# HGRN2 encoder layer on one core: x kept as rows until it is modulated, and the loads of the beginning in another order

## The chip, the cores and the metric

The kernel runs on 1 core of one Trainium2 chip. The metric is the time of one execution in microseconds on the device; lower is better. Times below are the median of three runs, and one execution was recorded by the hardware profiler.

## The reference

With DEPTH = 1 the trunk is one adaLN-modulated HGRN2 layer, then a final RMSNorm. It is applied to a prompt of 1024 rows and a sample of 256 rows (D = 1024, E = 2048, 16 heads).

```python
cs = jax.nn.silu(c)
shift, scale, gate = jnp.split(cs @ ada_w[0] + ada_b[0], 3, axis=-1)
h = _rms(x) * norm_g[0] * (1.0 + scale[:, None]) + shift[:, None]
q, f_fw, f_bw, i, z = jnp.split(h @ w_in, 5, axis=-1)
o = gated_chunkwise(q, ..., f_fw) + flip(gated_chunkwise(flip(q), ..., flip(f_bw)))
y = ((_rms(o) * norm_g_head) * jax.nn.silu(z)) @ w_out
x = x + gate[:, None] * y
return _rms(x) * final_g
```

## The kernel before, in words

The 1280 rows of x are ten row blocks of 128 (`xs[0]` to `xs[9]`), grouped in three segments `SEGS` of 512, 512 and 256 rows. The 1024 channels are eight blocks of 128; a channel pair r is blocks 2r and 2r+1. Everything later needs h with channels on the partitions, split into a high part `h_hi` and a low part `h_lo`, so that a product of fp32 accuracy is three fast ones: `hi*h_hi`, `hi*h_lo`, `lo*h_hi`. Weights are split in the same way by `split_w` (L113 to L119): ACT casts the high part, GpSimd subtracts for the low part. The high and low buffers are rings of three, the raw buffers a ring of two.

The program has three parts. The beginning (L229 to L327) makes h and, while h comes in, the products of the first two projections, q and ff of head 0. The main loop (L714 to L743) runs the other projections: the next one after the beginning is the value projection of heads 0 and 1 (`pv`, L444), ten tiles of 24 products. The tail is the output projection.

In the beginning, before the change, the order of all engines is the order of the code (`manual_schedule()`). A row block is loaded (`load_x`, ring of 4), normalised in place (`norm_x`: ACT square and root, DVE reciprocal and scaling), and transposed by TensorE into `xT` through PSUM (`transpose_x`; DVE copies one half, ACT the other). For a channel pair r, `mod_mm(r)` multiplies the conditioning by four pieces of `ada_w` (`aw`), `mod_tr(r)` transposes the result, and DVE finishes shift and scale (`mod`). `make_h(si, r)` then modulates `xT` in place, casts the high parts and subtracts the low ones. `first_project(r, accs)` adds a pair's products to the accumulators `p_acc[i, si]` (i = 0 for q, 1 for ff). Blocks 0 to 7 are transposed first, then come `mod_mm(0)` and the first products; the loop over r from 1 to 3 follows. Loads are issued by SP from the same code, so they stand between the blocks' work.

The eight PSUM banks have tags: `pj` (three), `tu` (two), `sc` (two) and `ob` (one). Before, the six accumulators take two `pj`, two `sc` and two `tu` banks, once the transposes are done.

```python
for r in range(1, 4):
    mod_mm(r)
    if r < 3:
        load_mod(r + 1)
    first_project(r - 1, ((0, 1),))
    mod_tr(r)
```

Of the kernel before, what the change touches and what calls it, by code (L numbers as in the profile page):

```python
# [45 lines left out]
def kernel(  # L46
# [99 lines left out]

    p0 = tc.alloc_tile_pool(name="p0", bufs=1)
    ada3 = ada_w[0].rearrange("(k p) n -> p k n", p=P)
    xT = [p0.tile([P, KT, sl], F32, name=f"xT{i}") for i, (_, sl) in enumerate(SEGS)]
    xts, p_acc, aws, raws, mrows = {}, {}, {}, {}, {}  # L150

    def load_x(j):
        xts[j] = p0.tile([P, D], F32, tag="xj", bufs=4, name=f"xj{j}")
        sp.dma_start(xts[j], xs[j])

    def load_mod(r, pieces=range(4)):

        for k0, i in [(0, 0), (0, 1), (4, 0), (4, 1)][pieces[0]:pieces[-1] + 1]:
            aws[r, k0, i] = p0.tile([P, 4, 256], F32, tag="aw", bufs=7, name=f"aw{r}_{k0}_{i}")
# [12 lines left out]

    def transpose_x(j):
        xj = xts[j]
        si = min(j // 4, 2)
        c = slice(j * P - SEGS[si][0], (j + 1) * P - SEGS[si][0])
        for h in range(2):
            xp = ps.tile([P, 512], F32, tag=("tu", "sc")[h], bufs=2, name=f"xp{j}_{h}")
            for i in range(4):
                k = 4 * h + i  # L180
                pe.transpose(xp[:, i * P:(i + 1) * P], xj[:, k * P:(k + 1) * P], ident)
            (act.copy if h else dve.tensor_copy)(
                xT[si][:, 4 * h:4 * h + 4, c], xp.rearrange("p (i c) -> p i c", i=4))
# [36 lines left out]
    def first_project(r, accs):  # L220

        for i, si in accs:
            hi, lo = ready[i]
# [4 lines left out]

    with tc.manual_schedule():  # L229
        crow = p0.tile([2 * KT, P], F32, name="crow")  # L230
        sp.dma_start(crow[:KT], c_prompt.rearrange("o (k p) -> (o k) p", p=P))
# [22 lines left out]
        def row(j):  # L254
            if j + 2 < 8:
                norm_x(j + 2)
            transpose_x(j)
            if j + 4 < NT:
                load_x(j + 4)

        norm_x(0)
        norm_x(1)
        for j in range(8):
            row(j)
            if j == 2:
                split(0, raws[0])
            if j == 3:
                load_mod(0)
                raws[1] = fetch_raw(1)
            if j == 5:  # L270
                load_mod(1, (0, 1, 2))
            if j == 6:
                split(1, raws[1])
        mod_mm(0)
        load_mod(1, (3,))
        mod_tr(0)
        make_h(0, 0)
        make_h(1, 0)
# [2 lines left out]
        norm_x(8)
        norm_x(9)
        first_project(0, ((0, 0), (1, 0)))
        row(8)
        row(9)
# [5 lines left out]
        for r in range(1, 4):
            mod_mm(r)
            if r < 3:
                load_mod(r + 1)
            first_project(r - 1, ((0, 1),))
            mod_tr(r)
            if r == 3:
                raws[2] = fetch_raw(2)
                wv = [split_w(*raws[2][0])]
            for si in range(3):  # L300
                make_h(si, r)
            first_project(r - 1, ((1, 1), (0, 2), (1, 2)))
            if r < 3:
                first_project(r, ((0, 0), (1, 0)))
        first_project(3, ((0, 0), (0, 1), (0, 2), (1, 0)))
# [540 lines left out]
```

## Time and profile before

| | us |
|---|---|
| median of three runs | 1708.84 |
| lowest, highest | 1707.33, 1713.25 |
| the profiled execution | 1708.66 |
| its span, first to last instruction | 1706.9 |
| TensorE busy | 1652.4 (97%) |
| DVE, ACT, GpSimd busy | 995.2, 803.0, 599.0 |
| mean granted TensorE clock | 0.993 |

The span is 1.8 us shorter than the execution's own time. A busy TensorE is not one at its peak: the granted clock tells which of its two levels it has, 1.2 GHz (0.50) or 2.4 GHz (1.00). In the rows, PE is TensorE, PEld its weight loads, POOL is GpSimd, and SP issues the loads.

### The profile page before, as it was taken

The page shows a single profiled execution, that of the slowest core. Times are in us where ns is not written, and L with a number is a line of the kernel's source. Part 1 is how long each engine was busy: PE and PEld are TensorE (multiplying, and loading weights), DVE is VectorE, ACT ScalarE, POOL GpSimd, SP SyncE. Part 2 cuts the span into 40 slices and gives each one's busy share as a digit, 9 for nine tenths or more (in the row PEclk, how much of TensorE's full clock was granted, in tenths as well). Part 3 has the DMA queues.
Part 4 walks back from the last instruction along what each step waited for, and adds up shares of the span by engine and source line. Part 5 has one row for each costly group of instructions (what it writes and reads, how often), then busy time and mean ns, then how long its engine had stood idle before and what let it go on. Part 6 is the DMA issues. An engine that isn't in the chain of part 4 may idle for free.

```text
span 1706.9 us, 28295 instructions
## 1 busy us (share of the span) xinstructions
PE 1652.4 (97%) x11511; PEld 1442.3 (84%) x11511; DVE 995.2 (58%) x2223; ACT 803.0 (47%) x1213; POOL 599.0 (35%) x547
## 2 busy tenths in 40 slices
PE   5999999999999999999999999999999999899998
PEld 4798789888988898889888998889888988788886
DVE  5647664757566745774576457644865476834322
ACT  6543634464545454544455445634563456542210
POOL 1533333343344333433344334433443334510000
PEclk8999999999999999999999999999999999999999
DMA  8312311011011011111111110111111100664310
GB/s 284 123 40 62 101 29 50 29 38 38 29 53 38 29 38 41 32 47 38 38 35 47 38 38 29 41 32 44 41 38 35 44 17 13 205 197 148 124 50 25
DMA packets 121268, 103.06 MB, mean 60 GB/s; under 512 B 3929, under 2 KB 108466, under 8 KB 121138
## 3 DMA queue, kind: packets, MB, share of 16 engines
q1 hardware_dynamic: 121138, 101.26, 18.9%
q8 instruction: 90, 1.47, 0.4%
q14 instruction: 40, 0.33, 0.1%
HBM read 85.50 MB, written 15.74 MB: 59 GB/s over the span
## 4 chain that ended last, share of the span: by engine, by line
PE 78%; DVE 9%; ACT 3%; POOL 3%; issue 2%; DMA 0%; DVEq 0%; POOLq 0%
PE pv L444 13%; PE y L690 13%; PE pff L422 13%; PE pfb L422 13%; PE pq L422 8%; PE pz L422 7%; PE ob L609 3%; DVE g L467 3%; PE up L532 3%; PE sc L553 2%; DVE kts L523 1%; PE kt L520 1%; DVE ku L474 1%; POOL wz_l L118 1%; PE sc L559 1%
## 5 line engine op out<-in xcount | busy, mean ns | idle before, releaser
L488 POOL TENSOR_TENSOR ku<-xx,dec 128x256 f32<-128x256 f32 (+1 forms) x96 | 82.0, 854 | 305.0 <-DVE dec L481 147.1
L444 PE MATMUL pv<-wv_h,h_hi 128*128 128x256 f32 x640 | 181.2, 283 | 0.0
L444 PE MATMUL pv<-wv_h,h_lo 128*128 128x256 f32 x640 | 181.1, 283 | 0.0
L444 PE MATMUL pv<-wv_l,h_hi 128*128 128x256 f32 x640 | 181.1, 283 | 0.0
L523 DVE COPY kts<-kt 128x512 f32<-128x512 f32 (+2 forms) x96 | 47.9, 499 | 198.0 <-PE kt L520 198.0
L422 PE MATMUL pz<-h_hi,wz_h 128*128 128x512 f32 (+1 forms) x384 | 144.4, 376 | 0.0
L422 PE MATMUL pq<-h_hi,wq_h 128*128 128x512 f32 (+1 forms) x360 | 139.1, 387 | 0.0
L422 PE MATMUL pff<-h_hi,wff_h 128*128 128x512 f32 (+1 forms) x360 | 138.5, 385 | 0.0
L422 PE MATMUL pfb<-h_hi,wfb_h 128*128 128x512 f32 (+1 forms) x384 | 136.3, 355 | 1.4 <-DVE q L406 1.4
L422 PE MATMUL pz<-h_hi,wz_l 128*128 128x512 f32 (+1 forms) x384 | 136.7, 356 | 0.0
L422 PE MATMUL pz<-h_lo,wz_h 128*128 128x512 f32 (+1 forms) x384 | 136.4, 355 | 0.0
L422 PE MATMUL pfb<-h_lo,wfb_h 128*128 128x512 f32 (+1 forms) x384 | 136.0, 354 | 0.0
L422 PE MATMUL pfb<-h_hi,wfb_l 128*128 128x512 f32 (+1 forms) x384 | 135.8, 354 | 0.0
L422 PE MATMUL pq<-h_hi,wq_l 128*128 128x512 f32 (+1 forms) x360 | 129.4, 359 | 0.0
L422 PE MATMUL pq<-h_lo,wq_h 128*128 128x512 f32 (+1 forms) x360 | 129.0, 358 | 0.0
L422 PE MATMUL pff<-h_hi,wff_l 128*128 128x512 f32 (+1 forms) x360 | 128.3, 356 | 0.0
L422 PE MATMUL pff<-h_lo,wff_h 128*128 128x512 f32 (+1 forms) x360 | 128.0, 356 | 0.0
L444 PEld LDWEIGHTS pv<-wv_l,h_hi 128*128 128x128 f32 x640 | 122.9, 192 | 0.0
L444 PEld LDWEIGHTS pv<-wv_h,h_lo 128*128 128x128 f32 x640 | 122.9, 192 | 0.0
L444 PEld LDWEIGHTS pv<-wv_h,h_hi 128*128 128x128 f32 x640 | 122.9, 192 | 0.0
L467 DVE TENSOR_TENSOR_SCAN g<-reset,g 128x512 f32<-128x512 uint8 (+1 forms) x96 | 101.8, 1073 | 24.6 <-ACT g L459 24.5
L397 POOL TENSOR_SCALAR k<-g,k_scale,k_bias 128x512 f32<-128x512 f32 (+1 forms) x96 | 75.0, 781 | 113.0 <-ACT g L395 104.3
(195 smaller groups left out, 4477.2 us busy)
## 6 DMA issues: line engine op xcount, KB each, us to landing
xj<-in_x_prompt_dram SPq DMA_DIRECT2D x16, 512.0 KB
wq_r<-in_hg_w_in_dram SPq DMA_DIRECT2D x16, 512.0 KB
aw<-in_ada_w_dram SPq DMA_DIRECT2D x16, 512.0 KB
wff_r<-in_hg_w_in_dram SPq DMA_DIRECT2D x16, 512.0 KB
wv_r<-in_hg_w_in_dram SPq DMA_DIRECT2D x16, 512.0 KB
wfb_r<-in_hg_w_in_dram SPq DMA_DIRECT2D x16, 512.0 KB
wz_r<-in_hg_w_in_dram SPq DMA_DIRECT2D x16, 512.0 KB
wo_r<-in_hg_w_out_dram SPq DMA_DIRECT2D x16, 512.0 KB
```

What stands on the lines that cost most here:

```text
L118: pool.tensor_tensor(lo, raw, hi.bitcast(F32), ALU.subtract)
L397: pool.tensor_scalar(k, g, k_scale[:, e:e + 1], k_bias[:, e:e + 1], ALU.mult, ALU.add)
L422: pe.matmul(acc[:, :sl], a[:, k, :], h[si][:, k, :], start=n == 0, stop=n == 3 * KT - 1)
L444: pe.matmul(acc[:, :2 * P], h[si][:, k, c], a[:, k % 4, :], start=n == 0, stop=n == 3 * KT - 1)
L467: dve.tensor_tensor_scan(gs, reset[:, :sl], gs, 0.0, ALU.mult, ALU.add)
L474: dve.tensor_tensor(chunks(ku), g3[:, :, last:last + 1].broadcast_to([P, nch, C]), g3, ALU.subtract)
L488: pool.tensor_tensor(u4[:, :, ca], x4[:, :, ca], dec[:, :, cb].broadcast_to([P, nb, C]), ALU.mult)
L523: dve.tensor_copy(kt[:, c], tp[:, c])
L532: pe.matmul(up[:, c], kt[:, c], v_t[e, b], start=True, stop=True)
L553: pe.matmul(sps[d][c * C:(c + 1) * C, i, c * C:(c + 1) * C], ke[:, o:o + C], qe[:, o:o + C], start=True, stop=True)
L609: pe.matmul(ob[:, c], l, r, start=n == 0, stop=n == len(ops) - 1)
L690: pe.matmul(y_bank(j, n), u[:, e % HALF, :], w[e][:, n * 512:(n + 1) * 512], start=first and e == 0, stop=last and e == NH - 1)
```

## The change

`xT`, `transpose_x` and the copies out of it are gone. A normalised row block stays as it is in its own buffer (ring of 10), and `make_h` now transposes what it needs, one channel block of one segment at a time, into a PSUM bank (`tu` for odd, `pj` for even channel blocks). ACT modulates from there straight into the high part, DVE modulates from there into a buffer `hv`, and the low part is `hv` less the high part, on GpSimd for even blocks and on DVE for odd ones. The accumulators of the sample segment share one bank `pf_2`, so one `tu` and one `pj` bank are left for the transposes. Only TensorE and SP keep the order of the code; a scheduler orders DVE, ACT and GpSimd by priority. The load list stands ahead of everything, with four pieces of modulation 1 ahead of row blocks 4 to 7, and the `aw` ring grows from 7 to 12. The lower-bound vector (`lbrow`) is loaded and transposed late. The second half of wv is split between the products instead of ahead of the last eighteen.

```diff
-        xts[j] = p0.tile([P, D], F32, tag="xj", bufs=4, name=f"xj{j}")
+        xts[j] = p0.tile([P, D], F32, tag="xj", bufs=10, name=f"xj{j}")
...
-        grp = 0 if SEGS[si][0] < TP else 1
-        hv = [xT[si][:, k, :] for k in (2 * r, 2 * r + 1)]
-        hi = [h_hi[si][:, k, :] for k in (2 * r, 2 * r + 1)]
-        lo = [h_lo[si][:, k, :] for k in (2 * r, 2 * r + 1)]
-        shift, scale = [[mod[:, s, k, grp:grp + 1] for k in (2 * r, 2 * r + 1)] for s in range(2)]
-        act.activation(hv[0], hv[0], AF.Identity, bias=shift[0], scale=scale[0])
-        dve.tensor_scalar(hv[1], hv[1], scale[1], shift[1], ALU.mult, ALU.add)
-        dve.tensor_copy(hi[0], hv[0])
-        act.copy(hi[1], hv[1])
-        pool.tensor_tensor(lo[0], hv[0], hi[0].bitcast(F32), ALU.subtract)
-        dve.tensor_tensor(lo[1], hv[1], hi[1].bitcast(F32), ALU.subtract)
+        s0, sl = SEGS[si]
+        grp = 0 if s0 < TP else 1
+        for k in (2 * r, 2 * r + 1):
+            xp = (tu_bank if k % 2 else pj_bank)(f"xp{si}_{k}")[:, :sl]
+            for i in range(sl // P):
+                pe.transpose(xp[:, i * P:(i + 1) * P], xts[s0 // P + i][:, k * P:(k + 1) * P], ident)
+            shift, scale = [mod[:, s, k, grp:grp + 1] for s in range(2)]
+            hi, lo = h_hi[si][:, k, :], h_lo[si][:, k, :]
+            hv = p0.tile([P, 512], F32, tag="hv", bufs=4, name=f"hv{si}_{k}")[:, :sl]
+            act.activation(hi, xp, AF.Identity, bias=shift, scale=scale)
+            dve.tensor_scalar(hv, xp, scale, shift, ALU.mult, ALU.add)
+            (dve if k % 2 else pool).tensor_tensor(lo, hv, hi.bitcast(F32), ALU.subtract)
...
-    with tc.manual_schedule():
+    with tc.manual_schedule(engines={PE, SP}):
...
         for j in range(4):
             load_x(j)
-        raws[0] = fetch_raw(0)
+        load_mod(0)
+        for i in range(2):
+            raws[i] = fetch_raw(i)
+        load_mod(1)
+        for j in range(4, 8):
+            load_x(j)
+        load_mod(2)
+        for j in range(8, NT):
+            load_x(j)
...
+        def products(r, si):
+            first_project(r, ((0, si), (1, si)))
+
+        for j in range(4):
+            norm_x(j)
+        mod_mm(0)
+        load_mod(3)
+        raws[2] = [fetch_raw(2)]
+        mod_tr(0)
+        split(0, raws[0])
+        split(1, raws[1])
+        make_h(0, 0)
+        products(0, 0)
+        mod_mm(1)
+        mod_tr(1)
+        for j in range(4, 8):
+            norm_x(j)
+        make_h(0, 1)
+        make_h(1, 0)
+        products(1, 0)
+        make_h(1, 1)
+        products(0, 1)
+        mod_mm(2)
+        products(1, 1)
+        mod_tr(2)
+        make_h(0, 2)
...
+        make_h(1, 2)
+        products(2, 0)
+        mod_mm(3)
+        make_h(2, 0)
+        products(2, 1)
+        mod_tr(3)
+        make_h(0, 3)
+        make_h(2, 1)
+        products(0, 2)
+        make_h(1, 3)
+        products(3, 0)
+        products(1, 2)
...
+        make_h(2, 2)
+        make_h(2, 3)
+        wv = [split_w(*raws[2][0][0])]
+        products(3, 1)
+        ready[2] = wv + [split_w(*raws[2][0][1])]
+        products(2, 2)
+        products(3, 2)
```

Three places show how the instructions moved. The first is ACT at the norms of row blocks 4 to 7 (`sq` is the square of a block, `rst` its root, `xp` a bank of transposes, `xT` the transposed x; the number behind a name is the block or segment). Before:

```order
L168 ACTIVATE sq4_188,ssum4_189<-xj4_165 128x1024
L169 ACTIVATE rst4_190<-ssum4_189,eps_t_71 128x1
L182 COPY xT0_98<-xp2_1_201 128x4x128
L117 CAST wq0_h_209<-wq0_r_120 128x1024
L168 ACTIVATE sq5_213,ssum5_214<-xj5_186 128x1024
L169 ACTIVATE rst5_215<-ssum5_214,eps_t_71 128x1
L182 COPY xT0_98<-xp3_1_226 128x4x128
L168 ACTIVATE sq6_244,ssum6_245<-xj6_207 128x1024
L169 ACTIVATE rst6_246<-ssum6_245,eps_t_71 128x1
L182 COPY xT1_99<-xp4_1_257 128x4x128
L168 ACTIVATE sq7_265,ssum7_266<-xj7_232 128x1024
L169 ACTIVATE rst7_267<-ssum7_266,eps_t_71 128x1
```

With the change:

```order
L168 ACTIVATE sq4_322,ssum4_323<-xj4_134 128x1024
L184 ACTIVATE h_hi0_89<-xp0_2_350,mod_81 128x512
L169 ACTIVATE rst4_324<-ssum4_323,eps_t_71 128x1
L168 ACTIVATE sq5_329,ssum5_330<-xj5_136 128x1024
L184 ACTIVATE h_hi0_89<-xp0_3_359,mod_81 128x512
L169 ACTIVATE rst5_331<-ssum5_330,eps_t_71 128x1
L168 ACTIVATE sq6_336,ssum6_337<-xj6_138 128x1024
L169 ACTIVATE rst6_338<-ssum6_337,eps_t_71 128x1
L168 ACTIVATE sq7_343,ssum7_344<-xj7_140 128x1024
L169 ACTIVATE rst7_345<-ssum7_344,eps_t_71 128x1
L184 ACTIVATE h_hi1_90<-xp1_0_368,mod_81 128x512
```

Between the norms stood copies of finished transposes; now there stand the modulating copies of channel blocks 2 and 3 of segment 0, which read `mod`, so the squares of blocks 5 to 7 come behind modulation 1.

The second is TensorE behind a modulation's small transpose (`pf0_0` is q's accumulator of segment 0). Before, at pair 0:

```order
L212 MATMUL mod_ps_130<-ident_66,mrow0_352 128x128
L226 MATMUL pf0_0_371<-h_hi0_89,wq0_h_209 128x512
L226 MATMUL pf0_0_371<-h_lo0_92,wq0_h_209 128x512
L226 MATMUL pf0_0_371<-h_hi0_89,wq0_l_210 128x512
L226 MATMUL pf0_0_371<-h_hi0_89,wq0_h_209 128x512
L226 MATMUL pf0_0_371<-h_lo0_92,wq0_h_209 128x512
```

With the change, behind the transposes for pair 1 of segment 0:

```order
L180 MATMUL xp0_3_359<-ident_66,xj3_112 128x128
L180 MATMUL xp1_0_368<-ident_66,xj4_134 128x128
L180 MATMUL xp1_0_368<-ident_66,xj5_136 128x128
L180 MATMUL xp1_0_368<-ident_66,xj6_138 128x128
L180 MATMUL xp1_0_368<-ident_66,xj7_140 128x128
L180 MATMUL xp1_1_377<-ident_66,xj4_134 128x128
L180 MATMUL xp1_1_377<-ident_66,xj5_136 128x128
L180 MATMUL xp1_1_377<-ident_66,xj6_138 128x128
L180 MATMUL xp1_1_377<-ident_66,xj7_140 128x128
L216 MATMUL pf0_0_165<-h_hi0_89,wq0_h_247 128x512
L216 MATMUL pf0_0_165<-h_lo0_92,wq0_h_247 128x512
L216 MATMUL pf0_0_165<-h_hi0_89,wq0_l_248 128x512
```

Products stood directly behind the modulation; now eight transposes of row blocks 4 to 7, for pair 0 of segment 1, stand ahead of pair 1's products of segment 0.

The third is ACT at the end of the beginning (`wv0_1` is the second half of wv, `q0` and `g0_0` the first results of q and ff). Before:

```order
L195 CAST h_hi1_90<-xT1_99 128x512
L192 ACTIVATE xT2_100<-xT2_100,mod_81 128x256
L195 CAST h_hi2_91<-xT2_100 128x256
L117 CAST wv0_1_h_742<-wv0_1_r_676 128x1024
L316 ACT_TABLE_LOAD
L316 ACTIVATE e0_758<-e0_758 128x16
L317 ACTIVATE e1_759<-e1_759 128x16
L117 CAST wfb0_h_891<-wfb0_r_889 128x1024
L405 ACTIVATE q0_0_792<-pf0_0_371 128x512
```

With the change:

```order
L184 ACTIVATE h_hi2_91<-xp2_7_711,mod_81 128x256
L316 ACTIVATE e1_763<-e1_763 128x16
L404 ACTIVATE q0_0_796<-pf0_0_165 128x512
L394 ACTIVATE g0_0_0_805<-pf1_0_167 128x512
L404 ACTIVATE q0_1_799<-pf0_1_166 128x512
L394 ACTIVATE g0_0_1_809<-pf1_1_168 128x512
L118 CAST wv0_1_h_734<-wv0_1_r_242 128x1024
L404 ACTIVATE q0_2_802<-pf_2_169 128x256
```

The cast of wv's second half stood ahead of all results of q and ff; now it stands behind those of segments 0 and 1.

## Rows read from the trace of the kernel before

**Rows 1.** The page, part 1: busy us, share of the span, instructions.

```profile
PE 1652.4 (97%) x11511; PEld 1442.3 (84%) x11511; DVE 995.2 (58%) x2223; ACT 803.0 (47%) x1213; POOL 599.0 (35%) x547
```

**Rows 2.** Stretches: us, busy PE, PEld, DVE, ACT, POOL (count), PEclk, DMA share, GB/s.

```profile
0.00:78.20 78.20, 55.77 (x487) 45.66 (x488) 47.43 (x86) 41.45 (x74) 25.21 (x23) 0.91 0.65 209
...
8.00:10.00 2.00, 0.00 (x0) 0.00 (x0) 0.51 (x2) 1.99 (x3) 0.00 (x0) 1.00 1.00 399
...
28.00:31.00 3.00, 2.19 (x65) 1.64 (x65) 0.59 (x3) 1.05 (x2) 0.00 (x0) 1.00 1.09 369
...
31.00:34.00 3.00, 0.00 (x0) 0.00 (x0) 2.96 (x3) 1.46 (x3) 2.34 (x1) 1.00 1.07 362
...
34.66:41.50 6.84, 6.04 (x17) 4.89 (x18) 5.49 (x9) 3.71 (x8) 2.04 (x2) 0.50 1.07 340
...
78.20:106.80 28.60, 28.60 (x240) 28.60 (x239) 22.59 (x55) 15.12 (x25) 12.65 (x21) 1.00 0.13 38
```

**Rows 3.** TensorE's timeline: start, us, engine, line, operation, count [idle before].

```profile
16.08 1.09 PE L181 MATMUL xp<-ident,xj 128*128 128x128 f32 x8 [0.97 <-DVE xT L182]
...
22.64 5.35 PE L181 MATMUL xp<-ident,xj 128*128 128x128 f32 x24 [2.33 <-DVE xT L182]
...
27.93 1.93 PE L204 MATMUL mod_ps<-aw,csT 128*2 128x128 f32 x64
...
30.30 0.33 PE L212 MATMUL mod_ps<-ident,mrow 128*128 128x128 f32 x1 [0.44 <-DVE mrow L208]
...
34.09 0.50 PE L226 MATMUL pf<-h_hi,wq_h 128*128 128x512 f32 x1 [3.46 <-DVE h_hi L194]
...
36.05 0.63 PE L226 MATMUL pf<-h_hi,wq_l 128*128 128x512 f32 x1
...
36.48 0.63 PE L226 MATMUL pf<-h_hi,wq_h 128*128 128x512 f32 x1
...
50.08 0.50 PE L226 MATMUL pf<-h_lo,wq_h 128*128 128x512 f32 x1 [0.67 <-POOL h_lo L196]
...
75.00 0.40 PE L226 MATMUL pf<-h_lo,wff_h 128*128 128x512 f32 x1
...
75.23 0.39 PE L226 MATMUL pf<-h_hi,wff_l 128*128 128x512 f32 x1
```

**Rows 4.** ACT's timeline, 10 to 50 us.

```profile
10.50 0.29 ACT L169 ACTIVATE rst<-ssum,eps_t 128x1 f32<-128x1 f32 x1
...
10.70 1.04 ACT L168 ACTIVATE sq<-xj 128x1024 f32<-128x1024 f32 x1
...
11.87 0.30 ACT L169 ACTIVATE rst<-ssum,eps_t 128x1 f32<-128x1 f32 x1
...
17.96 1.04 ACT L117 CAST wq_h<-wq_r 128x1024 fp32r<-128x1024 f32 x1
...
46.82 0.82 ACT L192 ACTIVATE xT<-xT,mod 128x512 f32<-128x512 f32 x1 [2.60 <-DVE mod L218]
```

**Rows 5.** DVE's timeline, 11 to 83 us.

```profile
11.02 0.75 DVE L171 TENSOR_SCALAR xj<-xj,rst 128x1024 f32<-128x1024 f32 x1
...
13.06 0.68 DVE L182 COPY xT<-xp 128x512 f32<-128x512 f32 x1
...
30.86 0.16 DVE L218 SCALAR_TENSOR_TENSOR mod<-mod,abT 128x4 f32<-128x4 f32 x1
...
31.06 2.64 DVE L193 TENSOR_SCALAR xT<-xT,mod 128x512 f32<-128x512 f32 x1
...
82.11 0.42 DVE L450 COPY vt<-pv 128x256 f32<-128x256 f32 x1
```

**Rows 6.** GpSimd's (POOL) timeline, 19 to 83 us.

```profile
19.09 2.36 POOL L118 TENSOR_TENSOR wq_l<-wq_r,wq_h 128x1024 fp32r<-128x1024 f32 x1 [17.72 <-ACT wq_h L117]
...
34.12 1.29 POOL L196 TENSOR_TENSOR h_lo<-xT,h_hi 128x512 fp32r<-128x512 f32 x1 [0.70 <-DVE h_hi L194]
...
80.18 2.42 POOL L118 TENSOR_TENSOR wfb_l<-wfb_r,wfb_h 128x1024 fp32r<-128x1024 f32 x1
```

More of the change, by code (lines that the diff above doesn't have):

```diff
@@ L16 @@
 PE = mybir.EngineType.PE
+SP = mybir.EngineType.SP
 PSUM = bass.MemoryType.PSUM
@@ L148 @@
     ada3 = ada_w[0].rearrange("(k p) n -> p k n", p=P)
-    xT = [p0.tile([P, KT, sl], F32, name=f"xT{i}") for i, (_, sl) in enumerate(SEGS)]
     xts, p_acc, aws, raws, mrows = {}, {}, {}, {}, {}
     def load_x(j):
-        xts[j] = p0.tile([P, D], F32, tag="xj", bufs=4, name=f"xj{j}")
+        xts[j] = p0.tile([P, D], F32, tag="xj", bufs=10, name=f"xj{j}")
         sp.dma_start(xts[j], xs[j])
@@ L158, in load_mod @@
         for k0, i in [(0, 0), (0, 1), (4, 0), (4, 1)][pieces[0]:pieces[-1] + 1]:
-            aws[r, k0, i] = p0.tile([P, 4, 256], F32, tag="aw", bufs=7, name=f"aw{r}_{k0}_{i}")
+            aws[r, k0, i] = p0.tile([P, 4, 256], F32, tag="aw", bufs=12, name=f"aw{r}_{k0}_{i}")
             sp.dma_start(aws[r, k0, i], ada3[:, k0:k0 + 4, i * D + r * 256:i * D + (r + 1) * 256])
@@ L171, in norm_x @@
         dve.tensor_scalar_mul(xj, xj, rst)
[L173 to L183, printed above, removed]
-    def make_h(si, r):
-        grp = 0 if SEGS[si][0] < TP else 1
-        hv = [xT[si][:, k, :] for k in (2 * r, 2 * r + 1)]
-        hi = [h_hi[si][:, k, :] for k in (2 * r, 2 * r + 1)]
-        lo = [h_lo[si][:, k, :] for k in (2 * r, 2 * r + 1)]
-        shift, scale = [[mod[:, s, k, grp:grp + 1] for k in (2 * r, 2 * r + 1)] for s in range(2)]
-        act.activation(hv[0], hv[0], AF.Identity, bias=shift[0], scale=scale[0])
-        dve.tensor_scalar(hv[1], hv[1], scale[1], shift[1], ALU.mult, ALU.add)
-        dve.tensor_copy(hi[0], hv[0])
-        act.copy(hi[1], hv[1])
-        pool.tensor_tensor(lo[0], hv[0], hi[0].bitcast(F32), ALU.subtract)
-        dve.tensor_tensor(lo[1], hv[1], hi[1].bitcast(F32), ALU.subtract)
+    def make_h(si, r):
+        s0, sl = SEGS[si]
[10 more added lines that the diff above has]
+            (dve if k % 2 else pool).tensor_tensor(lo, hv, hi.bitcast(F32), ALU.subtract)
     def mod_mm(r):
@@ L226, in first_project @@
                     pe.matmul(p_acc[i, si], a[:, k, :], h[si][:, k, :],
-                              start=k == n == 0, stop=k == KT - 1 and n == 2)
-    with tc.manual_schedule():
+                              start=k == n == 0 and (si < 2 or i == 0), stop=k == KT - 1 and n == 2,
+                              skip_group_check=si == 2)
+    with tc.manual_schedule(engines={PE, SP}):
         crow = p0.tile([2 * KT, P], F32, name="crow")
@@ L232 @@
         sp.dma_start(crow[KT:], c_sample.rearrange("o (k p) -> (o k) p", p=P))
-        lbrow = p0.tile([2 * NH + 1, P], F32, name="lbrow")
-        sp.dma_start(lbrow[:2 * NH], hg_lb.rearrange("l (h p) -> (l h) p", p=P))
-        sp.dma_start(lbrow[2 * NH:], hg_norm_g)
         abn = p0.tile([24, P], F32, name="abn")
@@ L240 @@
             load_x(j)
-        raws[0] = fetch_raw(0)
+        load_mod(0)
[7 more added lines that the diff above has]
+            load_x(j)
+        lbrow = p0.tile([2 * NH + 1, P], F32, name="lbrow")
+        sp.dma_start(lbrow[:2 * NH], hg_lb.rearrange("l (h p) -> (l h) p", p=P))
+        sp.dma_start(lbrow[2 * NH:], hg_norm_g)
         lb_ps = tu_bank("lb_ps")
@@ L252 @@
         dve.memset(mod_ps, 0.0)
[L254 to L278, printed above, removed]
         for i in range(2):
             p_acc[i, 0] = pj_bank(f"pf{i}_0")
[L281 to L285, printed above, removed]
-        for i in range(2):
-            p_acc[i, 1] = ps.tile([P, 512], F32, tag="sc", bufs=2, name=f"pf{i}_1")
-        make_h(2, 0)
-        for i in range(2):
-            p_acc[i, 2] = tu_bank(f"pf{i}_2")[:, :256]
@@ L291 @@
[L291 to L305, printed above, removed]
@@ L306 @@
-        ready[2] = wv + [split_w(*raws[2][1])]
-        first_project(3, ((1, 1), (1, 2)))
+            p_acc[i, 1] = ps.tile([P, 512], F32, tag="sc", bufs=2, name=f"pf{i}_1")
+        pf_2 = tu_bank("pf_2")
+        for i in range(2):
+            p_acc[i, 2] = pf_2[:, 256 * i:256 * (i + 1)]
+        def products(r, si):
[5 more added lines that the diff above has]
+        raws[2] = [fetch_raw(2)]
@@ new lines @@
+        mod_tr(0)
[16 more added lines that the diff above has]
+        make_h(0, 2)
+        for j in range(8, NT):
+            norm_x(j)
+        make_h(1, 2)
+        products(2, 0)
@@ new lines @@
+        mod_mm(3)
+        make_h(2, 0)
+        products(2, 1)
[6 more added lines that the diff above has]
+        products(1, 2)
+        pe.transpose(lb_ps2 := mod_ps[:, 128:128 + 2 * NH + 1], lbrow, ident[:2 * NH + 1, :2 * NH + 1])
+        dve.tensor_copy(lbT, lb_ps2)
+        make_h(2, 2)
[3 more added lines that the diff above has]
+        ready[2] = wv + [split_w(*raws[2][0][1])]
```

2 lines of the change are left out of this document (removed).

## The prediction

> **What bounds the kernel now.** I read the busy times first: TensorE works 97% of the span [rows 1], so a change pays only if TensorE reaches the later work sooner. Next the stretches [rows 2]. From 78.2 us on, with the first value projection, it is gapless (28.60 of 28.60 us, 240 matmuls, 0.119 us each); in the 78.2 us ahead it is busy 55.77, so 22.4 us are idle, all inside the part that the change rewrites. Behind that part both programs hold the same order on TensorE, and on the other engines it differs only in the first dozens of instructions. So the question is one number: when does the first value tile end? Before it is 78.2 + 24 x 0.119 = 81.1 us. Third, TensorE's timeline [rows 3] shows the two speeds: a 512-column product starts 0.43 us after the one ahead at half clock (36.05, 36.48) and 0.23 at full (75.00, 75.23); a transpose takes 5.35/24 = 0.22 or 1.09/8 = 0.14. From 34.7 to 41.5 us the granted clock was 0.50, that is 1.2 of 2.4 GHz, right after 3 us without one matmul [rows 2]. The first product waits until 34.09.
>
> **The landing.** The queue moved 399 GB/s of x and some 360 of the rest [rows 2], so 512 KB take 1.3 and 1.5 us. The list is now x blocks 0-3, four pieces of modulation 0, wq, wff, four of modulation 1, x blocks 4-7, four of modulation 2, blocks 8-9. With the first byte at 4 us that gives, as estimates: x 0-3 by 9.5, modulation 0 by 15.5, wq 17.0, wff 18.5, modulation 1 by 24.5, x 4-7 by 30, modulation 2 by 36, modulation 3 by 45.
>
> **Unchanged sums.** Products, modulation sums and transposes are as many as before (144, 4, 80). The moved rows of the lower-bound vector cost one transpose either way. The ten copies out of transposes on each of ACT and DVE go (0.68 us on DVE), and twelve casts on each engine go or turn into modulating copies; none of them ended a wait of TensorE after 34 us except through the chain below, so I cost that at nothing.
>
> **New operations.** ACT modulates from PSUM: not in the trace. Nearest is the same operation from SBUF, 0.82 us [rows 4]; the lower bound is a plain PSUM copy, DVE's 0.68. I take 0.82. DVE modulates from PSUM: a PSUM copy of that size took 0.68; the same operation from SBUF took 2.64 beside a GpSimd split, as it ended only with that [rows 5]. I take 0.68, since a PSUM copy at 82.11 took 0.42 for half the size [rows 5] while GpSimd ran a split from 80.18 to 82.60 [rows 6]. The Trainium skill (SBUF — State Buffer, Who interferes with whom) says that a DVE instruction with at most one SBUF input and outside its two-port modes does not contend with GpSimd; the row agrees. By the SBUF row instead the sum would grow as in the second rival.
>
> **The first block.** Modulation sum 0 starts at 15.5; it took 1.93 us at full clock [rows 3], and TensorE has then done two small transposes in 11 us. I scale by the transposes' 0.22/0.136 to 3.2 us: 18.7. From the end of the sum (27.93 + 1.93) to the finished modulation (30.86 + 0.16) it is 1.16 us [rows 3, 5]: 19.9. ACT 0.82, DVE 0.68: 21.4. GpSimd is in order: wq low part (cast 1.04 [rows 4], split 2.36 [rows 6], from 17.0: 20.4), then the low part of block pair 0 (1.29): 22.7, then wff's low part: 25.1. The last four of the twelve products follow at 0.43: **26.8**. Before, the third of the twelve starts at 36.05 and ten steps of 0.43 end them at 40.4, so at this point the change is ahead.
>
> **The hole.** Modulation sum 1 comes next (3.2: 30.0; finished modulation 31.2). TensorE then has 8 transposes of blocks 0-3, and behind them, ahead of twelve products that need nothing else, the 8 transposes of x blocks 4-7. Those wait for the norms. ACT's order, shown above, puts the squares of blocks 5, 6 and 7 behind modulating copies that wait for modulation 1. So from 31.2: two copies (1.64), three squares with 1.17 from square to root, four roots of 0.2 to 0.3 [rows 4], then reciprocal and scaling, 0.95 [rows 5]: 7.0 us in all, 38.2; five transposes at 0.22: products go on at **39.3**. TensorE is idle some 7 us there. That a runnable product does not pass a waiting instruction is seen at 50.08: the high-part product behind it had its operands and stood 0.67 us too [rows 3].
>
> **The rest.** From 39.3, at full clock: 84 products of 512 columns at 0.229 (19.2), 48 of 256 at 0.119 (5.7), two modulation sums (3.9), small transposes (0.9), 56 transposes at 0.14 (7.9), the value tile (2.9): 40.5 us. Stalls on top: two PSUM banks are left for transposes, one for even and one for odd channel blocks, each busy until DVE has read it. Where two sets follow each other behind a new modulation, the bank is free 0.72 (30.30 to 31.02 [rows 3, 5]) + 0.82 + 0.68 + 0.1 = 2.3 us after the small transpose, which together with the eight between covers 1.4: a wait of 0.9 for pair 2. For pair 3 the next set is half as long and waits at both banks, 1.4; the last two sets of segment 2, with copies of half the size taken at two thirds, 0.8; and 0.6 for a low part, as at 50.08. Last, wv's second half: its cast takes the buffer of wq, which the last stage now uses to within six short products (0.7 us) of its end. Cast 1.04, split 2.36 and 0.8 of waits, some of them behind GpSimd's new gate work, against 0.7 + 1.5 of cover: 2.0. Before, eighteen products stood between wq's last one and the value tile. Stalls: 0.9 + 1.4 + 0.8 + 0.6 + 2.0 = 5.7. Half clock after the hole, as at 36 us: twelve products at 0.2 more, 2.4. The tile ends at 39.3 + 40.5 + 5.7 + 2.4 = 87.9, against 81.1: **6.8 us later**. Nothing behind takes it up: TensorE is full there. The profiled execution took 1708.66 us (span 1706.9), 0.18 below the median; 1708.66 + 6.8 = 1715.5.
>
> **Rivals.** *The clock stays full.* If what little TensorE does keeps or brings the clock up, sum 0 ends at 17.4, wff's split at 24.1, products at 25.0, sum 1 at 26.9, modulation at 28.1, and products go on at 35.8; the tile ends at 35.8 + 40.5 + 5.7 = 82.0: +0.9, 1709.6, not slower by a measurable amount. [...] Against it: the 3 us without a matmul that ended in half clock [rows 2]. The Trainium skill (TensorE: Matmul & The Clock Gate, Part 1) puts the ramp's penalty under 1% of a typical span and advises against fitting a cold count; left out, the sum would be this rival's.
> *DVE's modulating copies block on GpSimd.* Then each of four waits on a bank grows by a low part, 1.3 us [rows 6]: +5.2, 1720.7. Against it: the copy at 82.11.
> *The stalls are covered.* Banks come free in time, wv's split runs ahead as the change says, and the clock is full: 82.0 - 5.7 = 76.3, 4.8 less, 1703.9. It needs ACT and DVE to clear a bank within 1.1 us, against 0.82 + 0.68 of rows, and the cast to be early, against the buffer.
>
> **Chances.** Forecast 0.56 (1712 to 1719), clock 0.25 (1707 to 1712), blocked 0.12 (1719 to 1723), covered 0.07 (1703 to 1707). A measurement of this kernel tells 0.3% (5.1 us) from no change: slower is above 1714.0, most of the first case and the whole third, 0.58; within 0.36; faster, below 1703.7, 0.06. The cheapest bounds together (ACT 0.68, no clock loss, half the stalls) give about -2 us, the dearest (half clock for a second stretch 2.4, landings 1 us late, blocked copies) about +15. 1706 to 1722 leaves out less than 2 in 10.
>
> **What would show it.** First product near 21 to 22 us instead of 34.09; then a hole on TensorE of 6 to 8 us near 31 to 39, ended by DVE's scaling of x blocks 4 to 7; half clock behind it; gaps of about 1 us at transposes waiting on DVE; 1 to 2 us at the first value tile on GpSimd's wv split; first value tile near 86 to 90 us and the trace behind it shifted as a whole. Wrong if the hole is under 3 us, if squares 5 to 7 run ahead of modulation 1, or if the stretch behind 90 us differs in length.

## The result, and the profile after

The change made the kernel slower: 1719.16 us in the median of five runs (1717.34 to 1722.12) against 1708.84 for five of before (1707.33 to 1713.25), a ratio of 1.0061 with an interval of 1.005 to 1.0073. That is 10.3 us more; the forecast was 6.7 more, 1715.5, with a range up to 1722. The profiled execution of after took 1721.28 us, 12.6 more than that of before, and is what the rows below show.

The page's first part answers to [rows 1]:

```profile
span 1719.6 us, 28281 instructions
...
PE 1656.8 (96%) x11511; PEld 1441.8 (84%) x11511; DVE 994.2 (58%) x2213; ACT 802.5 (47%) x1206; POOL 596.5 (35%) x547
```

As many TensorE instructions as before, 4.4 us more busy time, 12.7 us more span: the rest is waiting. The stretches answer to [rows 2] (the same columns):

```profile
0.00:86.69 86.69, 57.92 (x487) 43.76 (x488) 47.13 (x86) 40.12 (x69) 24.26 (x31) 0.90 0.58 189
...
28.00:30.00 2.00, 2.00 (x6) 1.52 (x6) 0.00 (x0) 0.38 (x2) 0.00 (x0) 0.50 1.02 406
...
44.00:46.00 2.00, 2.00 (x6) 1.61 (x6) 1.69 (x3) 0.95 (x2) 0.83 (x1) 0.50 1.09 347
...
92.00:94.00 2.00, 2.00 (x12) 2.00 (x11) 1.63 (x3) 1.97 (x4) 0.00 (x0) 0.50 0.69 202
...
106.00:126.00 20.00, 20.00 (x142) 18.81 (x141) 7.96 (x23) 4.07 (x7) 8.01 (x8) 1.00 0.24 67
```

The first value tile now starts at 86.69 instead of 78.22, with 28.8 us of idle TensorE ahead of it instead of 22.4, and the clock is at its lower level (0.50, 1.2 GHz) at three places. From 106 to 126 us TensorE is full (20.00 of 20 us), as it was before from 78.2 us on. TensorE's timeline (as [rows 3]) shows where the idle time lies:

```profile
22.57 0.51 PE L216 MATMUL pf<-h_hi,wq_h 128*128 128x512 f32 x1 [2.23 <-ACT h_hi L184]
24.76 0.80 PE L216 MATMUL pf<-h_lo,wq_h 128*128 128x512 f32 x1 [1.68 <-POOL h_lo L186]
...
27.62 0.80 PE L216 MATMUL pf<-h_lo,wq_h 128*128 128x512 f32 x1 [1.21 <-DVE h_lo L186]
...
31.33 2.90 PE L193 MATMUL mod_ps<-aw,csT 128*2 128x128 f32 x64
34.65 0.33 PE L201 MATMUL mod_ps<-ident,mrow 128*128 128x128 f32 x1 [0.43 <-DVE mrow L197]
...
39.14 0.30 PE L180 MATMUL xp<-ident,xj 128*128 128x128 f32 x1 [3.29 <-DVE xj L171]
41.16 0.47 PE L180 MATMUL xp<-ident,xj 128*128 128x128 f32 x1 [1.72 <-DVE xj L171]
...
43.86 0.78 PE L216 MATMUL pf<-h_hi,wq_h 128*128 128x512 f32 x1
...
59.14 1.09 PE L180 MATMUL xp<-ident,xj 128*128 128x128 f32 x8 [1.38 <-DVE hv L185]
70.84 0.66 PE L180 MATMUL xp<-ident,xj 128*128 128x128 f32 x4 [1.38 <-DVE hv L185]
80.34 0.89 PE L180 MATMUL xp<-ident,xj 128*128 128x128 f32 x4 [1.09 <-DVE hv L185]
...
90.36 0.39 PE L443 MATMUL pv<-wv_l,h_hi 128*128 128x256 f32 x1 [1.95 <-POOL wv_l L119]
```

The first product comes 11.5 us earlier than before (22.57 against 34.09). Then everything is given back: in the hole from 34.65 to 43.86 TensorE does hardly more than sixteen transposes, three sets of transposes wait for their bank, and the value tile waits 1.95 us for the low part of wv.

What holds the first block is seen on DVE and GpSimd. DVE's timeline:

```profile
19.34 2.30 DVE L207 SCALAR_TENSOR_TENSOR mod<-mod,abT 128x4 f32<-128x4 f32 x1
...
24.17 0.81 DVE L185 TENSOR_SCALAR hv<-xp,mod 128x512 f32<-128x512 f32 x1 [0.81 <-ACT h_hi L184]
25.01 2.55 DVE L186 TENSOR_TENSOR h_lo<-hv,h_hi 128x512 fp32r<-128x512 f32 x1
...
35.22 0.16 DVE L207 SCALAR_TENSOR_TENSOR mod<-mod,abT 128x4 f32<-128x4 f32 x1
...
37.21 1.79 DVE L171 TENSOR_SCALAR xj<-xj,rst 128x1024 f32<-128x1024 f32 x1
...
39.75 0.69 DVE L186 TENSOR_TENSOR h_lo<-hv,h_hi 128x512 fp32r<-128x512 f32 x1
...
42.07 0.75 DVE L171 TENSOR_SCALAR xj<-xj,rst 128x1024 f32<-128x1024 f32 x1
```

GpSimd's timeline:

```profile
19.29 2.34 POOL L119 TENSOR_TENSOR wq_l<-wq_r,wq_h 128x1024 fp32r<-128x1024 f32 x1 [17.92 <-ACT wq_h L118]
...
24.66 2.35 POOL L119 TENSOR_TENSOR wff_l<-wff_r,wff_h 128x1024 fp32r<-128x1024 f32 x1
```

The step that finishes modulation 0, 128 by 4 numbers, ran from 19.34 to 21.64, to the end of GpSimd's split of wq (19.29 to 21.63); alone it takes 0.16 (35.22). DVE's low part took 2.55 beside the split of wff and 0.69 alone. The modulating copy from PSUM at 24.17 overlaps GpSimd's low part and the start of wff's split, took 0.81 and was not held. A scaling from SBUF was: it took 1.79 at 37.21, beside GpSimd's low part of 37.18 to 38.44, and 0.75 at 42.07. Last, ACT's timeline, in the first block and over the hole:

```profile
18.16 1.04 ACT L118 CAST wq_h<-wq_r 128x1024 fp32r<-128x1024 f32 x1 [3.76 <-DMA wq_r<-in_hg_w_in_dram]
...
22.42 1.04 ACT L118 CAST wff_h<-wff_r 128x1024 fp32r<-128x1024 f32 x1
23.36 0.78 ACT L184 ACTIVATE h_hi<-xp,mod 128x512 fp32r<-128x512 f32 x1
...
35.48 0.78 ACT L184 ACTIVATE h_hi<-xp,mod 128x512 fp32r<-128x512 f32 x1 [7.10 <-PE xp L180]
...
36.34 1.04 ACT L168 ACTIVATE sq<-xj 128x1024 f32<-128x1024 f32 x1
...
37.38 0.76 ACT L184 ACTIVATE h_hi<-xp,mod 128x512 fp32r<-128x512 f32 x1
...
39.60 1.04 ACT L168 ACTIVATE sq<-xj 128x1024 f32<-128x1024 f32 x1
```

In the first block the cast of wff stands between the two modulating copies. Ahead of the hole ACT was idle for 7.10 us, since the copy that waits for modulation 1 stood ahead of the squares of x blocks 5 to 7. In e2 below, where ACT is free to take them, the same squares start at 28.84, 30.21 and 32.01.

### The profile page after: what moved, and what is told of

Its sections match the earlier page's. It is cut to its first block, busy times and chain, and to the rows that moved or that the text cites. A ratio compares the mean times of both kernels' runs of the same rounds, so it can differ in the third digit from the quotient of the medians.

```text
span 1719.6 us, 28281 instructions
## 1 busy us (share of the span) xinstructions
PE 1656.8 (96%) x11511; PEld 1441.8 (84%) x11511; DVE 994.2 (58%) x2213; ACT 802.5 (47%) x1206; POOL 596.5 (35%) x547
## 4 chain that ended last, share of the span: by engine, by line
PE 79%; DVE 10%; ACT 4%; POOL 3%; issue 2%; DMA 1%; SPq 0%; DVEq 0%; POOLq 0%; ACTq 0%
PE pv L443 13%; PE y L689 12%; PE pfb L421 12%; PE pff L421 12%; PE pq L421 7%; PE pz L421 7%; PE ob L608 3%; PE up L531 3%; DVE g L466 3%; PE sc L552 2%; PE pf L216 1%; DVE kts L522 1%; DVE ku L473 1%; PE kt L519 1%; POOL wz_l L119 1%
```

## The experiments

Two measures are used: the time of the runs, and the start of the first product with wfb in the trace, a point behind everything that the edits touch (107.0 us before, 119.2 after). From that point to the end the profiled spans of before and after are 1599.9 and 1600.4 us long. n is the number of runs; the ratio is to the kernel before on the same chip.

| kernel | first wfb product, us | median, us (n) | ratio, interval |
|---|---|---|---|
| the change | 119.2 | 1719.16 (5) | 1.0061, 1.005 to 1.0073 |
| e7 loads | 111.3 | 1714.10 (11) | 1.0029, 1.002 to 1.0038 |
| e2 ACT's order | 114.6 | 1716.04 (8) | 1.0037, 1.0024 to 1.0049 |
| e3 TensorE's order | 116.2 | 1719.10 (6) | 1.0061, 1.0048 to 1.0074 |
| e5 the lock | 115.3 | 1718.46 (5) | 1.0053, 1.0036 to 1.007 |
| e1 wv | 114.0 | 1718.64 (5) | 1.0052, 1.004 to 1.0064 |
| e6 banks | 116.3 | 1718.85 (5) | 1.0052, 1.0035 to 1.0068 |
| e9 the clock | 116.6 | 1719.76 (5) | 1.0058, 1.0043 to 1.0074 |
| e8 = e7 + e1 + e5 + e6 | 104.3 | 1706.57 (12) | 0.9988, 0.9975 to 1.0 |
| e10 = e8 without e6 | 108.7 | 1709.77 (11) | 1.0012, 1.0003 to 1.0021 |
| e11 = e8 without e1 | 108.1 | 1708.18 (11) | 0.9999, 0.999 to 1.0007 |
| e13 = e8 without e7 | 111.2 | 1711.19 (11) | 1.0021, 1.0012 to 1.003 |
| e12 = e8 and more order | 103.2 | 1704.61 (11) | 0.9981, 0.9971 to 0.9992 |

One profile is one execution. The cast of wq, which waits for its load, starts between 17.79 (e1) and 18.69 us (e6), and modulation sum 1 takes 1.93 us in some profiles (e1, e7) and 2.9 to 3.0 at half clock in others (after, e3, e6). So each term is also read between two marks of its own trace.

**The hole, by the load order (e7).**

```diff
-        load_mod(1)
         for j in range(4, 8):
             load_x(j)
+        load_mod(1)
         load_mod(2)
```

> Load order alone: x blocks 4 to 7 ahead of the four pieces of modulation 1. The scheduler then puts all four norms, ScalarE's and VectorE's parts, ahead of modulation 1. Theory (order): x blocks 4 to 7 land by about 25 us, modulation 1 by about 30.5, still ahead of its sum at 31.3; the hole behind modulation 1 falls from 8.5 us to the copies' own latency, products go on near 38.5, 5 us less than the changed kernel: 1714, range 1711 to 1716; if TensorE also keeps its full clock behind it, up to 2 us more. Rival (the banks and copies set the loss): under 1 us less. Rival (the later landing of modulation 1 costs as much as the earlier rows give): no difference.

Measured: 1714.10, and the hole is gone. TensorE's timeline of e7:

```profile
33.75 0.33 PE L201 MATMUL mod_ps<-ident,mrow 128*128 128x128 f32 x1 [0.42 <-DVE mrow L197]
33.92 1.04 PE L180 MATMUL xp<-ident,xj 128*128 128x128 f32 x8
36.26 1.09 PE L180 MATMUL xp<-ident,xj 128*128 128x128 f32 x8 [1.30 <-DVE hv L185]
37.11 0.48 PE L216 MATMUL pf<-h_hi,wq_h 128*128 128x512 f32 x1
```

From the small transpose to the next product it is 3.4 us instead of 9.2, 5.8 less, and the products run at full clock from there. The runs give 0.0032 of 1709 less, 5.5 us. So the theory of order holds, and the banks alone do not make the hole. The rival of a late modulation 1 does not show in this trace (it does in one of e11, below).

**The hole, by ACT's order alone (e2).**

```diff
-    with tc.manual_schedule(engines={PE, SP}):
+    with tc.manual_schedule(engines={PE, SP, ACT}):
...
         products(0, 1)
+
+    with tc.manual_schedule(engines={PE, SP}):
         mod_mm(2)
```

> ScalarE follows the order of the code up to the products of the first channel pair with segment 1, so that the squares and roots of x blocks 4 to 7 run before the copies that wait for modulation 1. TensorE's and the queue's orders stay; VectorE still scales the four blocks behind the finishing of modulation 1. Theory (order): the hole shrinks by ScalarE's part; four scalings of some 0.95 us follow the finished modulation at 35.4, so products go on near 39.5 to 40.5 instead of 43.9, 4 us less: 1715, range 1713 to 1717. Rival (the new operations from PSUM and the two banks set the loss): the four scalings were not the limit, under 1 us less.

Measured: 1716.04, 4.1 us less by the ratios, as expected. The squares of x blocks 4 to 7 now run from 27.46 to 33.16, and products go on 6.5 us behind the small transpose, 2.7 less. DVE's timeline tells what took over:

```profile
33.87 0.16 DVE L208 SCALAR_TENSOR_TENSOR mod<-mod,abT 128x4 f32<-128x4 f32 x1
...
36.72 0.75 DVE L172 TENSOR_SCALAR xj<-xj,rst 128x1024 f32<-128x1024 f32 x1
37.39 1.52 DVE L186 TENSOR_SCALAR hv<-xp,mod 128x512 f32<-128x512 f32 x2
```

The four scalings, 33.95 to 37.39, now stand ahead of the modulating copies, which release the bank that TensorE waits for (3.43 us at 38.25). ACT's order is about half of what e7 takes from the hole; DVE's scalings are what is left. Not all of the 4.1 us is the hole: in code order ACT casts wff ahead of both modulating copies (20.17), and modulation sum 1 starts 11.6 us behind the small transpose of modulation 0 instead of 12.7.

**The hole, by TensorE's order alone (e3).**

```diff
-        make_h(1, 0)
         products(1, 0)
+        make_h(1, 0)
         make_h(1, 1)
```

> On TensorE alone the twelve products of channel pair 1 with segment 0 stand ahead of the eight transposes of x blocks 4 to 7. Theory (TensorE's own order keeps runnable products behind waiting transposes): those products, 12 at 0.43 = 5.2 us at half clock, go into the hole; 1.7 us come back, as the copies of the transposes are no longer covered by them: 3.5 us less, 1715.7, range 1714 to 1718. Rival (those products were waiting for their own operands, and not for the transposes): within 1 us of the changed kernel.

Measured: 1719.10, no gain, outside the expected range. The products did start in the hole, at 36.30, but waited there for their own high and low parts (0.45, 1.69 and 1.03 us), and then a set of transposes waited 1.35 for its bank. From the small transpose of modulation 1 to the next modulation sum the trace has 15.7 us instead of 17.2: 1.5 gained of 3.5. The runs do not show even that. The profiled one, at 1724.17, has half clock at five later places, against two for after, and is 1606.3 us long behind the first wfb product. So this rival is half right: the products were held by the transposes and, right behind, by their own operands.

**GpSimd's lock (e5).** The addition for the scale now goes to unused columns of the modulation's PSUM bank, and the last step reads it from there.

```diff
-        dve.tensor_tensor(dst, tr.rearrange("p (s i r) -> p s i r", s=2, r=32)[:, :, :, 0:2],
-                          abT[:, :2, i2].broadcast_to([P, 2, 2, 2]), ALU.add)
-        dve.scalar_tensor_tensor(dst[:, 1], dst[:, 1], 1.0, abT[:, 2, i2].broadcast_to([P, 2, 2]),
-                                 ALU.add, ALU.mult)
+        tv = tr.rearrange("p (s i r) -> p s i r", s=2, r=32)
+        dve.tensor_tensor(dst[:, 0], tv[:, 0, :, 0:2], abT[:, 0, i2].broadcast_to([P, 2, 2]), ALU.add)
+        dve.tensor_tensor(tv[:, 1, :, 2:4], tv[:, 1, :, 0:2], abT[:, 1, i2].broadcast_to([P, 2, 2]), ALU.add)
+        dve.scalar_tensor_tensor(dst[:, 1], tv[:, 1, :, 2:4], 1.0, abT[:, 2, i2].broadcast_to([P, 2, 2]),
+                                 ALU.add, ALU.mult)
```

> The last step that finishes a modulation takes its first operand from a PSUM bank and not from SBUF, so it has one SBUF operand and not two; a small addition on VectorE comes with it. Theory (GpSimd's split of wq holds this VectorE step, which has two SBUF operands): in the changed kernel's trace it took 2.30 us for 128x4, from 19.34 to 21.64, while the split ran; now some 0.1 to 0.2 us, modulation 0 is finished near 19.8 and the first product starts near 21 instead of 22.57. The low parts on GpSimd and VectorE still come behind the splits (24.76 and 27.62), so the end of the first twelve products moves by under 0.5 us and the time by 0 to 1 us: 1718.7. Rival (the step waits for something else, or the lock takes hold at any VectorE step): still some 2 us there. Rival (the lock at this step carries through): 1.7 us less, 1717.5.

DVE's timeline of e5:

```profile
20.05 0.16 DVE L208 SCALAR_TENSOR_TENSOR mod<-mod_ps,abT 128x4 f32<-128x4 f32 x1
...
23.77 2.56 DVE L186 TENSOR_TENSOR h_lo<-hv,h_hi 128x512 fp32r<-128x512 f32 x1
```

and GpSimd's, the split beside which that step ran:

```profile
19.78 2.36 POOL L119 TENSOR_TENSOR wq_l<-wq_r,wq_h 128x1024 fp32r<-128x1024 f32 x1 [18.41 <-ACT wq_h L118]
```

0.16 us instead of 2.30: with one SBUF operand less the step is not held. The low part on DVE, with two, is held as before. From modulation 0's small transpose to the two products that wait for low parts it is 4.4 and 7.2 us instead of 6.1 and 9.0, so the 1.75 us carry through; I had expected under 0.5, since GpSimd's own low part, I thought, would wait for the split. It did not: in after GpSimd had been idle for 1.8 us when the copy came. The runs, 1718.46, cannot tell 1.7 us from none.

**The second half of wv (e1).**

```diff
-        products(3, 1)
+        first_project(3, ((0, 1),))
+        first_project(2, ((0, 2),))
+        first_project(3, ((0, 2),))
         ready[2] = wv + [split_w(*raws[2][0][1])]
-        products(2, 2)
-        products(3, 2)
+        first_project(3, ((1, 1),))
+        first_project(2, ((1, 2),))
+        first_project(3, ((1, 2),))
```

> Only the order of the products of the last channel pair changes: all that use wq come first, so that wq's buffer, which the second half of wv waits for, comes free some 2.1 us of TensorE work earlier. Theory (the order sets the loss): the 1.95 us stall of the first value tile goes, and with it the half clock in the 3 us behind it (about 1.4 us): 3.3 us less than the changed kernel, 1715.8, range 1714.5 to 1717.5. Rival (the split is late because of GpSimd's own queue, its gate work and memsets): stall stays within 0.3 us, time unchanged. Rival (the half clock at 91 us has another cause than the stall): 2 us less, and the half clock stays.

In the trace the value tile no longer waits, and no half clock follows: from the last transposes (80.34 in after, 78.13 here) to the first wfb product it is 35.9 us instead of 38.8, 3.0 less. The runs, 1718.64, lie outside the expected range and moved by less than their uncertainty.

**The banks (e6).** Three moves of this kind, for pairs 2 and 3 and for segment 2:

```diff
-        products(1, 1)
         mod_tr(2)
         make_h(0, 2)
+        products(1, 1)
```

> On TensorE twelve products now stand between two sets of transposes wherever these followed each other directly in the later part (pairs 2 and 3 and the last sets of segment 2). Theory (two banks, each read by ScalarE and VectorE before the next set): the three waits on VectorE's copies, 1.38, 1.38 and 1.09 us, go; some of it comes back where products then wait for a fresh copy: 2.5 to 3.8 us less, 1716, range 1715 to 1717.5. Rival (the products between come too early, their operands not ready: the same wait moves to the products): under 1 us less.

In the trace two of the three waits go and one of 1.03 stays; from modulation sum 2 to the value tile it is 31.2 us instead of 34.8, 3.6 less. The runs, 1718.85, are outside the expected range and again do not resolve it.

**The clock (e9).** `keep(n)` puts n transposes of the identity on TensorE, and the numbers in `products` do so between its products:

```diff
         make_h(0, 0)
-        products(0, 0)
+        keep(12)
+        products(0, 0, {0: 8, 3: 6})
...
         make_h(0, 1)
+        keep(18)
         make_h(1, 0)
```

> 44 transposes of the identity, whose results nobody reads, are added on TensorE in the beginning where it waits: 12 behind the transposes of pair 0, 8 and 6 at the two waits for low parts, 18 ahead of the transposes of x blocks 4 to 7. Theory (the half clock is a term of its own, besides the waits): the clock stays at 1.00 from 22 to 33 us and behind the hole, the first products and modulation sum 1 take 2.5 us less, the products behind the hole 2.4 us less: 4 us less, 1715, range 1714 to 1717. Rival (what half clock costs is hidden behind the waits): the records show full clock and the time falls by under 1 us. Rival (so few instructions do not hold the clock): half clock as before, time within 1 us or up to 2 us more.

TensorE's timeline of e9, the first products:

```profile
28.63 0.40 PE L216 MATMUL pf<-h_hi,wff_h 128*128 128x512 f32 x1
28.87 0.40 PE L216 MATMUL pf<-h_lo,wff_h 128*128 128x512 f32 x1
```

Here they start 0.23 us apart, full clock, against 0.43 in after (29.07, 29.50), and modulation sum 1 takes 1.93 instead of 2.90. The hole and the half clock behind it stayed. The first wfb product comes 2.6 us earlier, but the runs did not get shorter: 1719.76, outside the expected range. Nor does the sum alone show what the added transposes did, as it took 1.93 in e1 and e7 without them. So the clock in the first block is a real term of one trace, and what it is worth on average was not shown.

**All four (e8), and all four less one (e10, e11, e13).** Three single edits (e1, e6, e5) had moved the runs by less than their uncertainty, while the traces gave 3.0, 3.6 and 1.7 us.

> Four edits together: x blocks 4 to 7 loaded ahead of modulation 1, the last pair's products of wq first, the modulation's last step from PSUM, and products between the sets of transposes. Theory (order and waits set the loss, and its terms add): from the 12 us by which the first product with wfb was late (119.2 against 107.0), 6.0 for the hole and 3.0 for wv as their own runs showed, 0.5 for the lock and 3 for the banks: near 107, so the time of the kernel before within 2 us: 1709, range 1706 to 1711. Rival (a fixed cost of the new operations stays): 1713 or more.

Measured: 1706.57, 2.0 us under the kernel before with an interval that ends at none, and 12.5 under the change by the ratios. The marks in the traces add up to 5.8 + 1.75 + 3.0 + 3.6 = 14.1. Then one edit was left out each time:

> The four edits together, without the new load order, so that the norms of x blocks 4 to 7 again stand behind modulation 1. Theory (the hole is the largest term): 5 to 6 us more than with all four, 1.0022 of the kernel before, some 1712, with the waits for VectorE's scalings back at 5 to 7 us. Rival (the loss is spread over the other terms): 3 us or less.

> The four edits together, without the products between the sets of transposes (so the loads, wv and the modulation's last step stay edited). By the traces the three waits at the two banks are a term of 3.5 us, though the run with that edit alone gained under 1 us. Theory (the term is real, and a single edit's few runs were too few to show it): 3 to 3.5 us more than with all four, 1.0007 to 1.0012 of the kernel before instead of 0.9988, some 1710. Rival (those waits are taken up elsewhere): within 1 us of all four, 1707.

> The four edits together, without the new order of the last pair's products. Theory (late second half of wv: 1.95 us of waiting and about 1 us of half clock behind it): 3 us more than with all four, 1.0006 of the kernel before, some 1709.7, and the wait for GpSimd's wv split back at 2 us in the trace. Rival (the wait is hidden or costs no clock here): 1 to 2 us more.

Without the loads 0.0033 of 1709, 5.6 us more; without the banks' order 0.0024, 4.1 more. Their intervals do not touch that of e8; the first is what the theory said, the second a little more than its 3 to 3.5. Without wv's order it is 0.0011, 1.9 more: less than the theory's 3, and the intervals overlap, so the rival of a smaller term stands, though the traces give 2.9 (from the last transposes to the first wfb product 38.7 us, in e8 35.8). All four less the lock's edit (e5) was not run. TensorE's waits come back where expected, e13 (6.0 us with the three behind this one):

```profile
37.53 0.30 PE L180 MATMUL xp<-ident,xj 128*128 128x128 f32 x1 [3.48 <-DVE xj L171]
```

e10:

```profile
51.44 1.09 PE L180 MATMUL xp<-ident,xj 128*128 128x128 f32 x8 [1.57 <-DVE hv L185]
```

and e11, where modulation sum 1 also waited:

```profile
32.70 1.04 PE L193 MATMUL mod_ps<-aw,csT 128*2 128x128 f32 x28 [2.08 <-DMA aw<-in_ada_w_dram]
...
79.27 0.39 PE L444 MATMUL pv<-wv_l,h_hi 128*128 128x256 f32 x1 [1.93 <-POOL wv_l L119]
```

The first of these two rows is the price that e7's second rival named: with modulation 1 loaded behind x blocks 4 to 7, TensorE can reach its sum before the last piece has landed. The wait shows in this one profile, and in none of e7, e8, e10 and e12, which have the same load order.

**One step further (e12).** In pairs 0 and 1 of segment 0 the products with a low part of h come last, and segment 1's part of pair 0 stands around modulation sum 1:

```diff
-        products(0, 0)
-        mod_mm(1)
-        mod_tr(1)
+        late_lows(0, 0)
...
+        make_h(1, 0)
+        mod_mm(1)
+        first_project(0, ((0, 1),))
+        mod_tr(1)
         make_h(0, 1)
-        make_h(1, 0)
-        products(1, 0)
+        first_project(0, ((1, 1),))
+        late_lows(1, 0)
         make_h(1, 1)
-        products(0, 1)
```

> All four edits, and TensorE's order in the beginning: of the first twelve products of pairs 0 and 1 those that need a low part of h come last, and the transposes and products of pair 0 with segment 1 stand around modulation sum 1. Theory (what is left there is order as well): the waits of 1.4 and 1.2 us for low parts, which GpSimd's splits delay, go, and the products with segment 1 cover the finishing of modulation 1 (1.5 and 0.4 us of waiting): up to 4 us less than all four, 1703, range 1701 to 1706, and the first product with wfb near 100.5 instead of 104.3. Rival (modulation 1 lands too late, near 31 us, and TensorE only waits there instead): within 1 us of all four.

Measured: 1704.61, 3.2 us under the kernel before with an interval that leaves none out; 1.2 less than e8, of the 4 expected, and the two intervals overlap, so the runs do not tell e12 from e8. TensorE's timeline of e12:

```profile
25.77 0.50 PE L213 MATMUL pf<-h_hi,wff_l 128*128 128x512 f32 x1 [1.27 <-POOL wff_l L119]
...
28.04 0.33 PE L180 MATMUL xp<-ident,xj 128*128 128x128 f32 x1 [0.47 <-DVE xj L171]
...
30.76 3.24 PE L193 MATMUL mod_ps<-aw,csT 128*2 128x128 f32 x64
```

The waits for low parts became one for wff's low part, 1.27, and three for scalings, 1.53 together; and behind these waits the sum ran at half clock (0.52 and 0.63 granted from 30 to 34 us), 3.24 instead of 1.93. That the rest of the 4 us went there is read from one trace. The rival, a late landing of modulation 1, does not show as a wait here.

## Why the prediction was right, and where it was off

- **Where the time is decided.** Right: TensorE is full behind the value tile, and the trace there is shifted as a whole. The tile ended at 92.3 us (92.07 and one step of 0.21) against 81.1: 11.2 later, forecast 6.8. Half clock behind the tile, not forecast, is in the 1.5 by which the span grew beyond that. The range held the measured time with 2.8 us to spare, so a second miss as large as that of the first block would have left it.
- **The first block** is the step that failed. I had GpSimd in order, wff's split done at 25.1 and the last four of twelve products behind it, ended at 26.8. In the trace modulation sum 1 started at 31.33: 4.5 us late, the whole miss. 1.9 of it is the split, done at 27.01: wq landed later than estimated (cast at 18.16, not 17.0), and its split held the step that finishes modulation 0 to 21.64 (forecast 19.9). The other 2.6 is a step that my sum has no term for, DVE's low part of channel block 1: it came behind the cast of wff on ACT, was held by wff's split, and left eight products, not four, to start at 27.62. What I left out is thus that GpSimd's splits hold DVE steps with two SBUF operands, 2.30 and 2.55 us instead of 0.16 and 0.69, and that such a step stands ahead of products. e5 shows the first hold; the second, and the cast, are read from the traces of after and e2 and were not tried by themselves. I had weighed this lock for the modulating copies only, as the second rival, and they were indeed not held (0.81). The Trainium skill (SBUF — State Buffer, Who interferes with whom) states the other half as well: a DVE instruction with two SBUF inputs contends with a GpSimd instruction that reads SBUF. The trace agrees, with 2.30 beside the split and 0.16 without. I had used only the half on one input.
- **The sum and modulation 1.** 4.4 us forecast, 4.1 measured (31.33 to 35.38).
- **The hole.** 8.1 forecast (31.2 to 39.3), 8.5 measured (35.38 to 43.86), ended by DVE's scaling as foreseen. e7, e2 and e13 show its cause, the order of ACT and DVE behind modulation 1, worth 5.5 (e7) and 5.6 us (e13) by the runs.
- **The rest.** From there to the end of the tile 48.6 forecast, 48.4 measured. The three bank waits were 1.38, 1.38 and 1.09 (0.9, 1.4 and 0.8 forecast), wv's 1.95 (2.0); the 0.6 for a low part did not come. e10 shows that the bank waits are worth 4 us of the runs; wv's is seen in the traces and not resolved by the runs.
- **The half clock.** It came behind the hole as forecast (44 to 46 us at 0.50). There the first seven steps took 3.13 us, at 0.229 they would have taken 1.6. What it is worth in the runs was not tried by itself: e9 took the half clock out of the first block only, and there the runs did not get shorter.
- **The rivals.** The time, 1719.16, lies in the bin that I gave to blocked copies (1719 to 1723), but they did not block (0.81), and the clock did not stay full. "Covered", the faster side, is what e8 and e12 are: with the stalls covered the new operations are no loss. The loss was their order and, in the first block, GpSimd's hold, whose share the runs do not resolve.

## What to carry to other kernels

Where one engine keeps the order of the code and the others are ordered by a scheduler, look for the first instruction that waits for late data and list what stands behind it on each engine: here squares behind a modulating copy, scalings behind squares, products behind transposes, and 5 us with them. A low-part split on GpSimd is not free cover: here a DVE step with two SBUF operands that began while one ran ended only behind it, even one of 128 by 4 numbers (2.30 us), and one operand in PSUM freed it (0.16). When single edits are smaller than the runs can tell, put them together and leave one out at a time.

## What was not expected of the hardware

**The recorded clock can be wrong at the start.** In e8 the stretch from 24 to 28 us has a granted clock of 1.00:

```profile
24.00:28.00 4.00, 2.78 (x8) 1.69 (x7) 3.89 (x7) 3.90 (x9) 1.49 (x1) 1.00 1.09 351
```

but the products in it start 0.43 us apart, as at 1.2 GHz (TensorE's timeline of e8):

```profile
27.11 0.63 PE L217 MATMUL pf<-h_hi,wff_h 128*128 128x512 f32 x1
27.54 0.63 PE L217 MATMUL pf<-h_lo,wff_h 128*128 128x512 f32 x1
```

So the spacing of equal products is the safer reading. **The same wait does not always bring half clock.** The 1.9 to 2.0 us at the value tile stand in eight profiles; in six of them half clock followed, in two (e3 and e5) it did not. From that wait to the first wfb product it is 28.8 us in the six and 27.3 in the two, so half clock there costs 1.5 us, about what the lock's edit is worth, and a single profile does not price a term of that size.
